# Reordering fills, the last chunk's normalisation and the merge in a one-core decoder block

## The chip, the cores and the metric

The kernel runs on one core of one Trainium2 chip. The metric is device time in microseconds (us): the time of one execution of the whole program, inputs and outputs in device memory. The time of the kernel before is the median of three runs; beside it stands one profiled execution with its own time.

## The reference

All arrays are float32, batch 1, 1024 tokens, model width 1024. Cut to what matters here:

```
xn   = rmsnorm(x, norm_pre_g)
u_a, z_a, o_a, i_a, f_a, u_b, z_b, g_pre = split(xn @ w_in)

# branch a: four mLSTM heads of width 256, chunks of 128 tokens (eight chunks)
c = silu(causal_conv4(u_a));  q, k from c;  v from u_a          # per head
S = (q k^T) * decay                     # inside a chunk
h = (S v + inter * C_prev q) / max(|den|, exp(-m))
C = a * C_prev + (decayed v)(k)         # matrix state, carried from chunk to chunk
h = sigmoid(o_a) * h;  h = h * rsqrt(mean(h*h) + eps)           # per head and token
y_a = ((h * head_g + skip * c) * silu(z_a)) @ w_a_out
# branch b: complex diagonal state space, gated, projected
y_b = s5(u_b, z_b) @ w_b_out
# merge
merged = sigmoid(g_a) * y_a + sigmoid(g_b) * y_b
out    = x + rmsnorm(merged @ w_o, norm_post_g)
```

## The kernel before

Every large product is made of pairs of fp32r values: a weight or an activation w is split into a high part (a copy on ScalarE) and a low part (a subtraction), and `dot3` issues three matmuls, high*high, high*low, low*high (L182 to L184). A projection unit of 512 tokens by 128 channels over eight row blocks is 24 such matmuls of 512 columns.

**Order.** The order of all work is written out by hand. A *unit* is one block of a projection; `run` executes it: it first sends pending stores and weight fetches to the queue of SyncE (SP), then the loads of the next `look[0]` units in `fillers`, then whatever stands in `early`, then the body, then what an earlier unit has deferred (`defer`, `step2`). `fill(n)` runs the next n units of the list `fillers`. All DMAs are issued by SP, in program order.

**Weights.** `plan` lists the weight blocks in order of use. `fetch` loads the next block into raw buffers (`wr`, two), `pump` splits it into `wh` (ScalarE, L142) and `wl` (VectorE, L144; GpSimd for later pieces where `pl` is set), two buffers each. `take` hands a block to its user, and with `ahead` pumps the next one.

**Heads.** The loop at L1273 runs over four heads, the inner loop at L1301 over eight chunks. For chunk c, `attn_a(c)` makes the scores, the decayed keys (`ksh`, `ksl`) and the scaled queries; `attn_b(c)` multiplies them with the values and with the state of the chunks before, updates the state and starts the output `hr`. Chunk c+1's `attn_a` is issued ahead of chunk c's `attn_b`. In between stand fills, which for heads 0 to 2 are the projection units of the next head (`o_unit`, eight token blocks, 24 matmuls of 256 columns; each writes a `sow` tile, of which there are two, and stores it). Before the change a head's first chunks go: fill, `attn_a(0)`, fill, `attn_a(1)`, `attn_b(0)`, fill, fill, `attn_a(2)`, `attn_b(1)`. After the eighth chunk come the `late` units of the next head: `u` (the convolution), `k`, `v`, `u`, `v`.

**Normalisation.** For each chunk `attn_ss` squares `hr` on ScalarE; after every fourth chunk GpSimd makes the scale `ss` from it and `attn_c` (VectorE, L1174, four instructions) applies it. `attn_ss` is deferred by one unit, `attn_c` stands in `early` and so runs ahead of the unit after that. `attn_d` (L1184, transposes on TensorE into PSUM, then VectorE) and `attn_e` (ScalarE, GpSimd L1204) turn the four chunks into rows of the input of w_a_out; for heads 0 to 2 they are stored to `yh_d`, `yl_d` and loaded back during head 3 (`ystep`).

**y_a and the merge.** w_a_out is used in two parts: `ya_unit` multiplies its first six row blocks (heads 0 to 2), while head 3 still runs, and stores gate * result + 0.25 * branch b to `pa_d`; `mg_unit` multiplies the last two row blocks (k = 6, 7; block `ya3`), adds `pa_d`, and splits the result into `mh`, `ml` (ScalarE L1366, GpSimd L1367, deferred by one unit). Column blocks 0 to 5 of `ya_unit` run as fills of head 3; blocks 6 and 7 (block `("ya", 3)`) run after it, mixed with the merge units: ya, mg, mg, ya, mg, mg, ya, mg, mg, ya, and then ten more `mg`. Results of projections go to a ring of three PSUM banks (`bank`), those of the heads mostly to a ring of five (`mbank`). `wo_unit(i, t)` is the last projection, four column blocks i by eight token blocks t, 24 matmuls of 256 columns each; at i = 3 it makes the norm's scale on VectorE (L1391, L1392) and GpSimd (L1393, a power), and `finish` scales, adds x and stores.

The lines that issue the merge before the change:

```
for m, hf in ((0, 0), (1, 0), (0, 1), (1, 1)):
    yaf(m, hf); mgf(*todo.popleft()); mgf(*todo.popleft())
```

Of the kernel before, what the change touches and what calls it, by code (L numbers as in the profile page):

```python
# [36 lines left out]
def hybrid_block(ctx, tc, x, norm_pre_g, w_in, conv_w, conv_b, w_q, w_k, w_v, b_i, b_f, head_g,  # L37
# [1077 lines left out]
    def attn_b(h, c):  # L1115
        hf, cl = c // 4, c % 4
        sh, sl_, qh, ql, ksh, ksl = hst.pop((h, c))
        vh, vl = vt[h, hf][0][:, cl, :], vt[h, hf][1][:, cl, :]
# [4 lines left out]
        if c < NCH - 1:
            for m in range(2):
                pc = mbank()
                ms = slice(m * P, (m + 1) * P)
# [24 lines left out]
        hr = ht((P, DH), "hr", 5)  # L1151
        sg = so.pop((h, c))
        V.scalar_tensor_tensor(hr, sg, 1.0, o[:, :DH], op0=ALU.add, op1=ALU.mult)
        hrs = hst["hr"]
        hrs.append(hr)
        if c < NCH - 1:
            tt(cl_, cf, ch_.bitcast(F32), ALU.subtract)
            ctm["hl"] = (ch_, cl_)
        defer(lambda: attn_ss(c, sg, hr, hrs, rd, ss))

    def attn_ss(c, sg, hr, hrs, rd, ss):
        cl = c % 4
# [56 lines left out]
            SY.dma_start(yh[k][:, HS[hf]].bitcast(F32), yh_d[k * P:(k + 1) * P, HS[hf]])  # L1219
            SY.dma_start(yl[k][:, HS[hf]].bitcast(F32), yl_d[k * P:(k + 1) * P, HS[hf]])  # L1220

    yaux = {}

    def ya_pre(ct, hf, pool=None):
        rs = slice(ct * P, (ct + 1) * P)
        pool, a, b, n = (hp, "hlh", "hll", 5) if pool is None else (pool, "ft", "fpa", 7)
        t1 = pool.tile([P, 512], F32, tag=a, bufs=n, name="y_t1")
        SY.dma_start(t1, t1_d[rs, HS[hf]])
        gb = pool.tile([P, 512], F32, tag=b, bufs=n, name="y_gb")
        SY.dma_start(gb, gb_d[rs, HS[hf]])  # L1230
        yaux[ct, hf] = (t1, gb)

    def ya_unit(i, m, hf):
        if m == 0 and hf == 0 and i < 3:
            cur["ya"] = take(("ya", i), i > 0)
        ct = 2 * i + m
        rs = slice(ct * P, (ct + 1) * P)
        t1, gb = yaux.pop((ct, hf))
        o = bank()
        proj_cm(o, cur["ya"], m * P, yh, yl, HS[hf], ks=list(range(6)))  # L1240
        V.scalar_tensor_tensor(t1, t1, 1.0, o, op0=ALU.add, op1=ALU.mult)
        V.scalar_tensor_tensor(gb, gb, 0.25, t1, op0=ALU.mult, op1=ALU.add)
        store(pa_d[rs, HS[hf]], gb)
# [29 lines left out]
    for h in range(H):  # L1273
# [81 lines left out]

    def mg_unit(ct, hf):
        if ct == 0 and hf == 0:
            cur["ya3"] = take("ya3", False)
        t1, pr = maux.pop((ct, hf))
        o = bank()  # L1360
        proj_cm(o, cur["ya3"], ct * P, yh, yl, HS[hf], ks=[6, 7])
        V.scalar_tensor_tensor(t1, t1, 1.0, o, op0=ALU.add, op1=ALU.mult)
# [3 lines left out]
        A.activation(mh[ct, hf], t1, AF.Copy)  # L1366
        defer(lambda: PL.tensor_tensor(ml[ct, hf], t1, mh[ct, hf].bitcast(F32), op=ALU.subtract))  # L1367

    ob, xres = {}, {}
    sso = fp.tile([P, NCH, 4], F32, name="sso")  # L1370

    def wo_unit(i, t):
        if t == 0:
# [12 lines left out]
        jk = fp.tile([P, 256], F32, tag="fjk", bufs=2, name="fjk")  # L1386
        A.activation(jk, o[:, :256], AF.Square, accum_out=sso[:, t, i:i + 1])
        mul(ob[t][:, cs], o[:, :256], gpo[:, cs])
        if i == 3:
            s = fp.tile([P, 1], F32, tag="fs", bufs=4, name="fs")  # L1390
            V.tensor_reduce(s, sso[:, t, :], axis=mybir.AxisListType.X, op=ALU.add)  # L1391
            V.tensor_scalar(s, s, 1.0 / D, 4.0 * EPS, op0=ALU.mult, op1=ALU.add)  # L1392
            PL.tensor_tensor(s, s, halfm[:, 0:1], op=ALU.pow)  # L1393
            finish(t, s)

# [65 lines left out]
```

## Time and profile before

| | |
|---|---|
| median of 3 runs | 996.41 us (995.38 to 998.93) |
| the profiled execution: its own time | 994.43 us |
| its span, first to last instruction | 992.7 us |
| TensorE busy | 971.8 us (98%) |
| VectorE, ScalarE, GpSimd busy | 625.5, 351.8, 203.1 us |
| granted TensorE clock, mean | 0.999 |
| moved by DMA | 148.32 MB, mean 149 GB/s |

How to read the rows that follow. A row of the timeline has the start in us from the beginning of the span, the duration, the engine, the line of the kernel, the operation, out<-in by tile names, partitions by elements, and in brackets how long the engine had been idle and what ended that. A row of the groups has the busy time and the mean duration of one instruction in ns, and then the idle time of the engine ahead of them. A row of the chain has start, duration and what it was. PE is TensorE, DVE VectorE, ACT ScalarE, POOL GpSimd, SPq the queue of SyncE. Matmuls overlap: a matmul of 512 columns shows about 0.40 us, but the next one starts earlier than that.

### The profile page before, as it was taken

To read this page: it belongs to the slowest core of one execution; us is meant where nothing else is said; L and a number is where in the kernel's file an instruction comes from. 1 tells how busy PE (TensorE), PEld (TensorE's weight loads), DVE (VectorE), ACT (ScalarE), POOL (GpSimd) and SP (SyncE) were. 2 spreads that over 40 slices of the span, in tenths; PEclk is the share of its full clock that TensorE was granted. 3 is DMA by queue.
4 is the path that set the end of the run, shared out by engine and by line. 5 is a ranking of instruction groups with operands and counts; after the bars stand their busy time and mean duration, and the time that the engine had idled before them with its cause. 6 is when DMAs were issued, how large, how long until landed. Compare 5 with 4: busy or idle time off the path is not lost.

```text
span 992.7 us, 15204 instructions
## 1 busy us (share of the span) xinstructions
PE 971.8 (98%) x5617; PEld 836.6 (84%) x5617; DVE 625.5 (63%) x1396; ACT 351.8 (35%) x696; POOL 203.1 (20%) x214
## 2 busy tenths in 40 slices
PE   7999999999999999999999999999999999999997
PEld 6878878888887789978998898889987888779997
DVE  4437978889644752435686667747774888765226
ACT  7312132331214421234544445435543442123311
POOL 4013222211122000012111321223221311343001
PEclk9999999999999999999999999999999999999999
DMA  7445323423334566114344253335446896783504
GB/s 256 111 130 158 112 88 97 109 58 107 108 100 164 185 216 226 59 64 151 96 133 152 85 173 122 134 95 179 130 151 189 270 312 204 268 299 121 191 1 170
DMA packets 115450, 148.32 MB, mean 149 GB/s; under 512 B 19080, under 2 KB 71472, under 8 KB 115376
## 3 DMA queue, kind: packets, MB, share of 16 engines
q1 hardware_dynamic: 115376, 147.35, 46.4%
q8 instruction: 44, 0.72, 0.3%
q14 instruction: 30, 0.25, 0.1%
HBM read 100.88 MB, written 46.43 MB: 148 GB/s over the span
## 4 chain that ended last, share of the span: by engine, by line
PE 85%; DVE 4%; DMA 4%; issue 3%; ACT 2%; POOL 1%; SPq 1%; DVEq 0%; POOLq 0%; ACTq 0%
PE pp L182 23%; PE pp L184 23%; PE pp L183 23%; PE pm L184 4%; PE pm L182 3%; PE pm L183 3%; DVE wl L144 1%; DMA wr<-in_w_in_dram 1%; PE pm L1088 1%; PE pm L664 1%; PE pm L705 1%; PE pm L704 1%; PE pm L1011 1%; DMA xt<-in_x_dram 1%; DMA ft<-t_d 1%
## 5 line engine op out<-in xcount | busy, mean ns | idle before, releaser
L182 PE MATMUL pp<-xh,wh 128*128 128x512 f32 x768 | 306.3, 399 | 3.3 <-DVE xl L278 2.5
L184 PE MATMUL pp<-xh,wl 128*128 128x512 f32 x768 | 303.6, 395 | 2.2 <-DVE wl L144 2.2
L183 PE MATMUL pp<-xl,wh 128*128 128x512 f32 x768 | 303.4, 395 | 0.2 <-DMA xl<-yl_d 0.2
L182 PEld LDWEIGHTS pp<-xh,wh 128*128 128x128 f32 x768 | 144.1, 188 | 39.9 <-DVE xl L278 2.8
L184 PEld LDWEIGHTS pp<-xh,wl 128*128 128x128 f32 x768 | 144.1, 188 | 37.9 <-DVE wl L144 3.1
L183 PEld LDWEIGHTS pp<-xl,wh 128*128 128x128 f32 x768 | 144.2, 188 | 33.2 <-DMA xl<-yl_d 0.7
L144 POOL TENSOR_TENSOR wl<-wr,wh 128x1024 fp32r<-128x1024 f32 (+1 forms) x25 | 61.6, 2481 | 227.3 <-ACT wh L142 227.3
L142 ACT ACTIVATE wh<-wr 128x1024 fp32r<-128x1024 f32 (+2 forms) x76 | 73.2, 1009 | 41.5 <-PE pm L183 30.6
L144 DVE TENSOR_TENSOR wl<-wr,wh 128x1024 fp32r<-128x1024 f32 (+2 forms) x51 | 59.9, 1207 | 21.7 <-ACT wh L142 17.2
L184 PE MATMUL pp<-wh,ml 128*128 128x256 f32 x256 | 72.2, 282 | 0.5 <-POOL ml L1367 0.5
L182 PE MATMUL pp<-wh,mh 128*128 128x256 f32 x256 | 72.1, 282 | 0.0
L183 PE MATMUL pp<-wl,mh 128*128 128x256 f32 x256 | 72.0, 281 | 0.0
L182 PE MATMUL pp<-wh,xh 128*128 128x256 f32 (+1 forms) x256 | 72.0, 281 | 0.0
L184 PE MATMUL pp<-wh,xl 128*128 128x256 f32 (+1 forms) x256 | 71.8, 280 | 0.0
L183 PE MATMUL pp<-wl,xh 128*128 128x256 f32 (+1 forms) x256 | 71.8, 280 | 0.0
L290 ACT ACTIVATE tg<-pp 128x512 f32<-128x512 f32 x32 | 19.2, 600 | 137.3 <-PE pp L184 94.3
L985 POOL TENSOR_TENSOR hll<-t2k,hlh 128x512 fp32r<-128x512 f32 x16 | 20.7, 1297 | 165.7 <-ACT hlh L984 89.1
L184 PEld LDWEIGHTS pp<-wh,ml 128*128 128x128 f32 x256 | 48.2, 188 | 0.7 <-POOL ml L1367 0.7
L182 PEld LDWEIGHTS pp<-wh,mh 128*128 128x128 f32 x256 | 48.2, 188 | 0.3 <-ACT mh L1366 0.2
L183 PEld LDWEIGHTS pp<-wl,xh 128*128 128x128 f32 x256 | 48.2, 188 | 0.2
L183 PEld LDWEIGHTS pp<-wl,mh 128*128 128x128 f32 x256 | 48.2, 188 | 0.1
L182 PEld LDWEIGHTS pp<-wh,xh 128*128 128x128 f32 x256 | 48.0, 188 | 0.2
(395 smaller groups left out, 1797.4 us busy)
## 6 DMA issues: line engine op xcount, KB each, us to landing
wr<-in_w_in_dram SPq DMA_DIRECT2D x48, 512.0 KB
t_d<-tg SPq DMA_DIRECT2D x32, 256.0 KB
xt<-in_x_dram SPq DMA_DIRECT2D x8, 512.0 KB
aux<-t_d SPq DMA_DIRECT2D x16, 256.0 KB
gb_d<-aux SPq DMA_DIRECT2D x16, 256.0 KB
so_d<-sow SPq DMA_DIRECT2D x32, 128.0 KB
sz_d<-t2k SPq DMA_DIRECT2D x16, 256.0 KB
cs_d<-t2k SPq DMA_DIRECT2D x16, 256.0 KB
```

What stands on the lines that cost most here:

```text
L142: A.activation(hi, raw, AF.Copy)
L144: eng.tensor_tensor(wl[:, k0:k0 + n, c0:c0 + w], raw, hi.bitcast(F32), op=ALU.subtract)
L182: PE.matmul(o, lh, rh, start=first, stop=False)
L183: PE.matmul(o, lh, rl, start=False, stop=False)
L184: PE.matmul(o, ll, rh, start=False, stop=last)
L290: A.activation(t, o, AF.Tanh, scale=0.5)
L664: PE.matmul(o[NS * b2:NS * (b2 + 1), g * P:(g + 1) * P], q["wt"][:, ri, g, NS * b2:NS * (b2 + 1)], ut[b][:, 2 * g + b2, :], start=True, st ...
L704: PE.matmul(o, m0[:, 2 * g + b2, :], ut[b][:, 2 * g + b2, :], start=True, stop=False)
L705: PE.matmul(o, vs[:, b2, g].rearrange("p t n -> p (t n)"), ss_[:, b2, g, :], start=False, stop=True)
L985: PL.tensor_tensor(lo, acc, hi.bitcast(F32), op=ALU.subtract)
L1011: PE.matmul(pm[:, 256 * k:256 * k + 256], wt[:, e, 256 + P * k:256 + P * k + P], wt[:, e, 0:256], start=e == 0, stop=e == 1)
L1088: PE.matmul(sc[:, :P], k_[:, m, sl], q_[:, m, sl], start=m == 0, stop=m == 1)
```

## The change

Nothing is added to or taken from the matmuls. The parts:

- **Chunk 0 of heads 0 to 2.** Two fills run ahead of `attn_a(1)` and `attn_b(0)` in place of one, and the fill after `attn_b(0)` goes; the count of fills per head stays.
- **Chunk 7 of each head.** `attn_ss` runs at once in place of being deferred by a unit, so `attn_c` runs ahead of the first unit after it. For head 2, `attn_d` of the second half then stands one unit earlier (after the `k` unit in place of the first `v` unit).
- **Blocks 6 and 7 of y_a.** Their `ya_unit` leaves its sum open in PSUM (`last=False`) and `mg_unit` goes on in the same bank. Their two VectorE instructions, their store to `pa_d` and the loads back go; the merge of these two reads gate and branch b from the tiles that the `ya_unit` loaded (`fyt`, `fyg`).
- **Order of the merge.** Two `ya`, six `mg`, two `ya`, six `mg`, then the last four `mg` in pairs between the first two `wo_unit`. Loads are issued four units ahead in place of three.
- **Weights.** The second piece of `ya3` is split on GpSimd; the fetch of the second w_o block comes after the merge's second run; its split one `wo_unit` later.
- **The norm.** Three of the four partial sums are added on VectorE one column block earlier; at i = 3 GpSimd adds the last one, and the two VectorE instructions there go. The squares' unused output has one buffer in place of two.

```diff
+        if c == NCH - 1:
+            attn_ss(c, sg, hr, hrs, rd, ss)
+        else:
+            defer(lambda: attn_ss(c, sg, hr, hrs, rd, ss))
...
-        pool, a, b, n = (hp, "hlh", "hll", 5) if pool is None else (pool, "ft", "fpa", 7)
+        pool, a, b, n = (hp, "hlh", "hll", 5) if pool is None else (pool, "fyt", "fyg", 2)
...
-        proj_cm(o, cur["ya"], m * P, yh, yl, HS[hf], ks=list(range(6)))
+        proj_cm(o, cur["ya"], m * P, yh, yl, HS[hf], ks=list(range(6)), last=i < 3)
+        if i == 3:
+            maux[ct, hf] = (t1, gb, o)
+            return
...
-            fill()
+            fill(2 if c == 0 and h < H - 1 else 1)
...
-            if c % 4 != 3 if h < H - 1 else c in (2, 4, 6):
+            if c in ((1, 2, 4, 5, 6) if h < H - 1 else (2, 4, 6)):
                 fill()
...
-            if i == (3 if h < H - 2 else 2):
+            if i == (3 if h < H - 2 else 1):
                 attn_d(h, 1)
...
-    cur["ya"] = take(("ya", 3))
+    cur["ya"] = take(("ya", 3), False)
+    pump(pl=True)
...
-        pr = fp.tile([P, 512], F32, tag="fpa", bufs=7, name="fpa")
+        pr = fp.tile([P, 512], F32, tag="fpa", bufs=5, name="fpa")
...
-        t1, pr = maux.pop((ct, hf))
-        o = bank()
-        proj_cm(o, cur["ya3"], ct * P, yh, yl, HS[hf], ks=[6, 7])
+        t1, pr, o = maux.pop((ct, hf))
+        part = o
+        o = bank() if part is None else part
+        proj_cm(o, cur["ya3"], ct * P, yh, yl, HS[hf], ks=[6, 7], first=part is None)
         V.scalar_tensor_tensor(t1, t1, 1.0, o, op0=ALU.add, op1=ALU.mult)
-        tt(t1, t1, pr, ALU.add)
+        if part is None:
+            tt(t1, t1, pr, ALU.add)
+        else:
+            V.scalar_tensor_tensor(t1, pr, 0.25, t1, op0=ALU.mult, op1=ALU.add)
...
-        A.activation(jk, o[:, :256], AF.Square, accum_out=sso[:, t, i:i + 1])
+        A.activation(jk, o[:, :256], AF.Square, scale=1.0 / 32.0, accum_out=sso[:, t, i:i + 1])
         mul(ob[t][:, cs], o[:, :256], gpo[:, cs])
+        if i == 2:
+            V.tensor_reduce(sso[:, t, 4:5], sso[:, t, 0:3], axis=mybir.AxisListType.X, op=ALU.add)
+            V.tensor_scalar(sso[:, t, 4:5], sso[:, t, 4:5], 4.0 * EPS, None, op0=ALU.add)
         if i == 3:
-            V.tensor_reduce(s, sso[:, t, :], axis=mybir.AxisListType.X, op=ALU.add)
-            V.tensor_scalar(s, s, 1.0 / D, 4.0 * EPS, op0=ALU.mult, op1=ALU.add)
+            PL.tensor_tensor(s, sso[:, t, 3:4], sso[:, t, 4:5], op=ALU.add)
             PL.tensor_tensor(s, s, halfm[:, 0:1], op=ALU.pow)
...
-    todo = deque((ct, hf) for hf in range(2) for ct in range(KT))
-    for m, hf in ((0, 0), (1, 0), (0, 1), (1, 1)):
-        yaf(m, hf)
-        mgf(*todo.popleft())
-        mgf(*todo.popleft())
-    for ct, hf in todo:
+    yaf(0, 0)
+    yaf(1, 0)
+    for ct in (6, 7, 0, 1, 2, 3):
+        mgf(ct, 0)
+    yaf(0, 1)
+    yaf(1, 1)
+    n_ya = len(fillers)
+    for ct, hf in ((6, 1), (7, 1), (4, 0), (5, 0), (0, 1), (1, 1)):
         mgf(ct, hf)
-    look[0] = 3
+    n_hf = len(fillers) - n_ya
+    for ct in range(2, 6):
+        mgf(ct, 1)
+    look[0] = 4
...
-    fill(10)
+    fill(n_ya)
     pump()
-    fill(4)
+    pending.pop()
+    fill(n_hf)
+    pending.append(fetch)
     for t in range(NCH):
         run(unit(lambda: wo_unit(0, t)))
-        fill(3)
-        if t == 1:
+        fill(2)
+        if t == 2:
             pump()
```

More of the change, by code (lines that the diff above doesn't have):

```diff
@@ L1158, in attn_b @@
             ctm["hl"] = (ch_, cl_)
-        defer(lambda: attn_ss(c, sg, hr, hrs, rd, ss))
+        if c == NCH - 1:
+            attn_ss(c, sg, hr, hrs, rd, ss)
+        else:
+            defer(lambda: attn_ss(c, sg, hr, hrs, rd, ss))
     def attn_ss(c, sg, hr, hrs, rd, ss):
@@ L1220, in ystep @@
             SY.dma_start(yl[k][:, HS[hf]].bitcast(F32), yl_d[k * P:(k + 1) * P, HS[hf]])
-    yaux = {}
+    yaux, maux = {}, {}
     def ya_pre(ct, hf, pool=None):
         rs = slice(ct * P, (ct + 1) * P)
-        pool, a, b, n = (hp, "hlh", "hll", 5) if pool is None else (pool, "ft", "fpa", 7)
+        pool, a, b, n = (hp, "hlh", "hll", 5) if pool is None else (pool, "fyt", "fyg", 2)
         t1 = pool.tile([P, 512], F32, tag=a, bufs=n, name="y_t1")
@@ L1345, in hybrid_block @@
     mh, ml = {}, {}
-    maux = {}
     def mg_pre(ct, hf):
@@ L1351, in mg_pre @@
         SY.dma_start(t1, t1_d[rs, HS[hf]])
-        pr = fp.tile([P, 512], F32, tag="fpa", bufs=7, name="fpa")
+        pr = fp.tile([P, 512], F32, tag="fpa", bufs=5, name="fpa")
         SY.dma_start(pr, pa_d[rs, HS[hf]])
-        maux[ct, hf] = (t1, pr)
+        maux[ct, hf] = (t1, pr, None)
     def mg_unit(ct, hf):
-        if ct == 0 and hf == 0:
+        if "ya3" not in cur:
             cur["ya3"] = take("ya3", False)
-        t1, pr = maux.pop((ct, hf))
-        o = bank()
-        proj_cm(o, cur["ya3"], ct * P, yh, yl, HS[hf], ks=[6, 7])
+        t1, pr, o = maux.pop((ct, hf))
+        part = o
+        o = bank() if part is None else part
+        proj_cm(o, cur["ya3"], ct * P, yh, yl, HS[hf], ks=[6, 7], first=part is None)
         V.scalar_tensor_tensor(t1, t1, 1.0, o, op0=ALU.add, op1=ALU.mult)
-        tt(t1, t1, pr, ALU.add)
+        if part is None:
+            tt(t1, t1, pr, ALU.add)
+        else:
+            V.scalar_tensor_tensor(t1, pr, 0.25, t1, op0=ALU.mult, op1=ALU.add)
         mh[ct, hf] = fp.tile([P, 512], F32R, name=f"mh{ct}{hf}")
@@ L1369, in hybrid_block @@
     ob, xres = {}, {}
-    sso = fp.tile([P, NCH, 4], F32, name="sso")
+    sso = fp.tile([P, NCH, 5], F32, name="sso")
     def wo_unit(i, t):
@@ L1385, in wo_unit @@
         cs = slice(256 * i, 256 * (i + 1))
-        jk = fp.tile([P, 256], F32, tag="fjk", bufs=2, name="fjk")
-        A.activation(jk, o[:, :256], AF.Square, accum_out=sso[:, t, i:i + 1])
+        jk = fp.tile([P, 256], F32, tag="fjk", bufs=1, name="fjk")
+        A.activation(jk, o[:, :256], AF.Square, scale=1.0 / 32.0, accum_out=sso[:, t, i:i + 1])
         mul(ob[t][:, cs], o[:, :256], gpo[:, cs])
+        if i == 2:
+            V.tensor_reduce(sso[:, t, 4:5], sso[:, t, 0:3], axis=mybir.AxisListType.X, op=ALU.add)
+            V.tensor_scalar(sso[:, t, 4:5], sso[:, t, 4:5], 4.0 * EPS, None, op0=ALU.add)
         if i == 3:
             s = fp.tile([P, 1], F32, tag="fs", bufs=4, name="fs")
-            V.tensor_reduce(s, sso[:, t, :], axis=mybir.AxisListType.X, op=ALU.add)
-            V.tensor_scalar(s, s, 1.0 / D, 4.0 * EPS, op0=ALU.mult, op1=ALU.add)
+            PL.tensor_tensor(s, sso[:, t, 3:4], sso[:, t, 4:5], op=ALU.add)
             PL.tensor_tensor(s, s, halfm[:, 0:1], op=ALU.pow)
@@ L1403, in mgf @@
     def mgf(ct, hf):
-        fillers.append(unit(lambda: mg_unit(ct, hf), lambda: mg_pre(ct, hf)))
+        fillers.append(unit(lambda: mg_unit(ct, hf), lambda: (ct, hf) in maux or ct > 5 or mg_pre(ct, hf)))
     def yaf(m, hf):
         fillers.append(unit(lambda: ya_unit(3, m, hf), lambda: ya_pre(6 + m, hf, fp)))
-    todo = deque((ct, hf) for hf in range(2) for ct in range(KT))
-    for m, hf in ((0, 0), (1, 0), (0, 1), (1, 1)):
-        yaf(m, hf)
-        mgf(*todo.popleft())
-        mgf(*todo.popleft())
-    for ct, hf in todo:
-        mgf(ct, hf)
-    look[0] = 3
-    for i in range(3):
+    yaf(0, 0)
[6 more added lines that the diff above has]
+    for ct, hf in ((6, 1), (7, 1), (4, 0), (5, 0), (0, 1), (1, 1)):
+        mgf(ct, hf)
+    n_hf = len(fillers) - n_ya
+    for ct in range(2, 6):
+        mgf(ct, 1)
+    look[0] = 4
+    for i in range(4):
         fillers[i][0]()
         fillers[i] = (None,) + fillers[i][1:]
-    fill(10)
+    fill(n_ya)
     pump()
-    fill(4)
+    pending.pop()
+    fill(n_hf)
+    pending.append(fetch)
     for t in range(NCH):
         run(unit(lambda: wo_unit(0, t)))
-        fill(3)
-        if t == 1:
+        fill(2)
+        if t == 2:
             pump()
```

## The prediction

> **What bounds the kernel now.** I read the page's first parts, then the waits of TensorE, then the timeline around each of them.
>
> ```profile
> span 992.7 us, 15204 instructions
> ...
> PE 971.8 (98%) x5617; PEld 836.6 (84%) x5617; DVE 625.5 (63%) x1396; ACT 351.8 (35%) x696; POOL 203.1 (20%) x214
> ```
>
> TensorE is busy for 98% of the span, and the change takes no matmul away. Only TensorE's waits can be won, and the tail after its last matmul. These are the waits that the change touches, in TensorE's timeline, with four successive matmuls that give a wait's price:
>
> ```profile
> 474.05 0.36 PE L182 MATMUL pm<-vh,ksh 128*128 128x258 f32 x1 [0.65 <-issue]
> ...
> 576.58 0.39 PE L182 MATMUL pm<-vh,ksh 128*128 128x258 f32 x1 [0.74 <-ACT ksh L1102]
> ...
> 577.40 0.39 PE L184 MATMUL pm<-vh,ksl 128*128 128x258 f32 x1 [0.31 <-DVE ksl L1107]
> ...
> 679.47 0.39 PE L182 MATMUL pm<-vh,ksh 128*128 128x258 f32 x1 [0.75 <-ACT ksh L1102]
> ...
> 680.28 0.39 PE L184 MATMUL pm<-vh,ksl 128*128 128x258 f32 x1 [0.32 <-DVE ksl L1107]
> ...
> 766.51 1.46 PE L1184 MATMUL pm<-ident,hr 128*128 128x128 f32 x8 [1.46 <-DVE hr L1174]
> ...
> 794.91 0.50 PE L183 MATMUL pp<-xl,wh 128*128 128x512 f32 x1 [0.17 <-DMA xl<-yl_d]
> ...
> 855.41 0.39 PE L183 MATMUL pp<-xl,wh 128*128 128x512 f32 x1
> 856.78 0.50 PE L184 MATMUL pp<-xh,wl 128*128 128x512 f32 x1 [0.98 <-DVE wl L144]
> 857.11 0.40 PE L182 MATMUL pp<-xh,wh 128*128 128x512 f32 x1
> 857.35 0.40 PE L183 MATMUL pp<-xl,wh 128*128 128x512 f32 x1
> 859.00 0.50 PE L184 MATMUL pp<-xh,wl 128*128 128x512 f32 x1 [1.26 <-DVE wl L144]
> ...
> 883.53 0.50 PE L182 MATMUL pp<-xh,wh 128*128 128x512 f32 x1 [0.23 <-DVE ft L1362]
> ...
> 888.42 0.39 PE L184 MATMUL pp<-wh,ml 128*128 128x256 f32 x1 [0.51 <-POOL ml L1367]
> ...
> 892.14 0.50 PE L182 MATMUL pp<-xh,wh 128*128 128x512 f32 x1 [0.53 <-DVE ob L442]
> ```
>
> A matmul of 512 columns follows the one before after 0.24 us (857.11 to 857.35). Around the first `wl` wait it is 1.37 (855.41 to 856.78), and 0.33 for the next: 1.22 lost for 0.98 shown. So a wait costs its bracket plus 0.25. That makes 0.90 at head 0's chunk 0, 1.55 and 1.57 at those of heads 1 and 2, 1.71 at head 2's `attn_d`, 0.42 at the load of `yl_d`, 2.74 for `ya3`'s two low pieces, 0.48, 0.76 and 0.78 later in the merge: 10.9 us, 1.1% of the span. That is the ceiling, before the tail.
>
> **Chunk 0, two fills ahead.** The fill brought forward stands between head h's first scores and the matmuls that wait for `ksh`, `ksl`. Rows of head 2:
>
> ```profile
> 677.83 0.68 DVE L442 TENSOR_TENSOR vl<-pp,vh 128x512 fp32r<-128x512 f32 x1
> ...
> 683.44 0.69 DVE L442 TENSOR_TENSOR ctl<-ct,cth 128x516 fp32r<-128x516 f32 x1
> ```
> ```profile
> 677.90 0.60 PE L1088 MATMUL pm<-q,k 128*128 128x128 f32 x4
> ...
> 681.23 0.28 PE L182 MATMUL pp<-wh,xh 128*128 128x256 f32 x1
> ...
> 686.88 0.38 PE L1088 MATMUL pm<-q,k 128*128 128x128 f32 x2
> ```
> ```profile
> 670.69 3.60 DMA wr<-in_w_in_dram
> ```
> ```profile
> 681.13 0.88 SPq L82 DMA_DIRECT2D so_d<-sow  x2
> ```
> ```profile
> 681.17 0.31 ACT L1096 ACTIVATE sTh<-sT 128x128 fp32r<-128x128 f32 x1 [0.96 <-DVE sT L442]
> ```
>
> Two fills now run from 681.23 to 686.88, so one is 2.8 us. The moved one would begin at 677.90, and `ksl` (needed by 680.28 now) would be asked for at about 681.3: the old wait is covered by 1 us. But the fill itself gets new waits. Its PSUM bank, third in the ring of three, is that of the last `v` unit, whose `vl` VectorE reads until 678.51: 0.6 late, with the price 0.7 (estimate; head 1 alike, head 0 none, its VectorE is ahead). Second, it is the third writer of `sow`, of which there are two, so ScalarE must wait until the first one's store, issued at 681.13, has landed. No row shows this landing; it lies between the issue and, at worst like the load of 512 KB, four times its size, 3.60 later, at 684.7. Behind that wait on ScalarE stand `sTh`, `ksh`, `q2h` and the state's copies of the next chunk; from `sTh` to the end of `ctl` it now takes 2.96 (681.17 to 684.13). ScalarE comes to `sTh` at 682.4, when the later scores allow it, or at 685.5, when the store lands last and two instructions (0.8, an estimate) go first; so `ctl` is done at 685.3 to 688.5. TensorE asks for it after another fill, scores and values, at about 687.8. So 0 to 0.9 is lost here; I take 0.3, nearer the early end, since the store is small. SP itself moves nothing by this: its order stays, and the cs_d store and the loads of `cz` keep their place. Gain: 0.90 + (1.55 - 1.0) + (1.57 - 1.0) = 2.0, between 0.9 and 4.0.
>
> **Chunk 7 at once, `attn_d` earlier.**
>
> ```profile
> 760.09 0.69 DVE L442 TENSOR_TENSOR hll<-pp,hlh 128x512 fp32r<-128x512 f32 x1 [4.54 <-ACT hlh L952]
> ...
> 764.93 2.21 DVE L1174 TENSOR_SCALAR hr<-hr,ss 128x256 f32<-128x256 f32 x4
> ```
> ```profile
> 762.17 0.20 POOL L1165 TENSOR_SCALAR ss<-ss 128x4 f32<-128x4 f32 x1 [18.96 <-ACT so L1163]
> ```
> ```profile
> 789.51 5.36 DMA xl<-yl_d
> ```
>
> Now `attn_c` ends at 767.1, behind the convolution on VectorE. Moved, its chain (the square, three small GpSimd operations) begins right after chunk 7's `hr`, and the four instructions fall into VectorE's idle 4.54 ahead of 760.09. The transposes then stand one `v` unit earlier (24 matmuls of 256 columns, 2.8) and ask at about 762.2: ready two microseconds before. What is queued behind `attn_c` is the next `u` unit's `hll` at 760.09; if the cover went, that unit's bank would be read 1 to 2 later, with two banks still free. So 1.71 goes. The stores of `yh_d`, `yl_d` and the loads behind them on SP move forward with `attn_d` by one unit, more than the 1.71 by which TensorE comes earlier, so the 0.42 at the landing (789.51 + 5.36) goes too. Gain 2.1, between 1.0 and 2.1. In the other heads `attn_d` keeps its place: nothing.
>
> **The merge.**
>
> ```profile
> L142 ACT ACTIVATE wh<-wr 128x1024 fp32r<-128x1024 f32 x66 | 66.6, 1054 | 30.6 <-PE pm L183 19.7 <-PE pp L183 7.0 <-DMA wr<-in_w_in_dram 3.3
> ...
> L1367 POOL TENSOR_TENSOR ml<-ft,mh 128x512 fp32r<-128x512 f32 x16 | 23.8, 1510 | 23.4 <-ACT mh L1366 23.4
> ...
> L144 DVE TENSOR_TENSOR wl<-wr,wh 128x1024 fp32r<-128x1024 f32 x42 | 52.8, 1289 | 21.7 <-ACT wh L142 17.2 <-PE pm L184 4.5
> ...
> L442 DVE TENSOR_TENSOR ft<-ft,fpa 128x512 f32<-128x512 f32 x16 | 13.3, 829 | 0.6
> ...
> L1366 ACT ACTIVATE mh<-ft 128x512 fp32r<-128x512 f32 x16 | 10.1, 633 | 34.6 <-DVE ft L442 34.6
> ...
> L1362 DVE SCALAR_TENSOR_TENSOR ft<-ft,pp 128x512 f32<-128x512 f32 x16 | 10.9, 684 | 2.6 <-DMA ft<-t_d 2.3 <-PE pp L184 0.3
> ```
> ```profile
> 854.41 4.54 DVE L144 TENSOR_TENSOR wl<-wr,wh 128x1024 fp32r<-128x1024 f32 x2
> ...
> 875.71 1.82 DVE L442 TENSOR_TENSOR ft<-ft,fpa 128x512 f32<-128x512 f32 x1
> ...
> 889.19 0.69 DVE L1362 SCALAR_TENSOR_TENSOR ft<-ft,pp 128x512 f32<-128x512 f32 x1 [1.96 <-DMA ft<-t_d]
> ```
>
> `ya3`'s low pieces are done at 858.95 and asked for from 855.6, after one `ya` unit. A second `ya` unit in front (18 matmuls by 0.235, 4.2) asks for them at 859.9, and GpSimd takes one of the two pieces. Even if VectorE's piece ended only at 859, the 2.74 goes.
>
> What is late next is VectorE. A merge unit is six matmuls, 1.40; VectorE's pair on it is 0.68 + 0.83 = 1.51. Before, a `ya` unit after every two gave it time; now six merge units come in a row. The first run ends in 8.4 us of `ya` units, in which VectorE has nothing to do: no loss. The second run starts with w_o's split, which gets its buffer when the last `ya` unit ends: ScalarE 1.05, then VectorE 2 x 1.29, so the first pair starts 3.6 after that. The fourth unit's bank, which `wo_unit` takes, is free at 3.6 + 3 x 1.51 + 0.68 = 8.8, asked for at 8.4: 0.65 with the price. Its `ml` is ready at 3.6 + 4 x 1.51 + 0.63 + 1.51 = 11.8; `wo_unit` wants it as the 18th matmul (0.118 apart), at 11.1: 0.95. So 1.6 in place of 0.48 + 0.76 + 0.78 = 2.02.
>
> Four stores and eight loads of 256 KB go, 3 MB, and none of the loads waits for a store of this stage any more, so the late load of 889.19 goes. Against it, the loads of the first run now stand behind w_o's fetch on SP, which waits for `ya3`'s split. They would land near 865 (a landing takes 5.4 above), and the first bank that hangs on one is asked for at 866.4 (859.4 and five merge units): nothing, up to 1 us. VectorE's dropped instructions are no gain by themselves. Merge: 2.74 + 2.02 - 1.6 = 3.2, between 0 and 4.8.
>
> **The norm's tail.**
>
> ```profile
> 986.71 0.19 ACT L1387 ACTIVATION_READ_ACCUMULATOR fjk<-pp 128x1 f32 x1
> ```
> ```profile
> 987.75 0.54 POOL L1393 TENSOR_TENSOR fs<-fs,halfm 128x1 f32<-128x1 f32 x1 [2.31 <-DVE fs L1392]
> ```
>
> Between 986.90 and the power at 987.75 lie 0.85 of VectorE's work and hand-over. A GpSimd add takes its place; it is not shown, at most as long as the power, 0.54, plus 0.1 of hand-over. Gain 0.2 to 0.75; I take 0.4. The two VectorE instructions at i = 2 and the single square buffer, which ScalarE alone writes, cost nothing beside 24 matmuls.
>
> **Sum.** 2.0 + 2.1 + 3.2 + 0.4 = 7.7 us. The profiled execution's 994.43 becomes 986.7; the median of the runs, 996.41, lies 1.98 above it, so a median of 988.7.
>
> **Rivals.**
> - *VectorE and GpSimd shut each other out in the merge.* The add of 875.71 took 1.82 against 0.69 at best, while GpSimd made an `ml`. If each pair took 0.68 + 1.82 = 2.5 against TensorE's 1.40 with three banks, the first run loses about 1.3, the second 5.0, together 6.3 in place of my 1.6: 993.4. For it: in a run of six, `ml` follows `ml`. Against it: the mean add is 0.83.
>   The Trainium skill, page "SBUF — State Buffer", section "SBUF: two separate sides", speaks for it: it calls the port pair of VectorE and GpSimd an exclusive lock, held for a whole instruction, when VectorE reads two SBUF inputs; the add does, the operation on PSUM does not. The trace agrees for the add of 1.82, and its mean says that the full price is rare.
> - *Chunk 0 gains nothing*: the two new waits take what the old one gave: 990.7.
> - *The waits only move*, to the next late engine, all over: 996.4. Against it: VectorE is busy for 63%.
> - *Slower: ScalarE hangs on the `so_d` store.* If it lands like the load of `yl_d` or later, `ctl` comes at 681.13 + 5.36 + 0.8 + 2.96 = 690.3 in place of 687.8: 2.5 lost per head. It decides for slower only if three heads lose over 3.6 more than I take, a landing after 6.8 or so: three times 4.0 gives 988.7 + 12 = 1000.7. Against it: the store has little ahead of it in the queue.
>
> **How the numbers follow.** The forecast, 985 to 991.5: 0.66. Shut out in the merge: 0.10. Chunk 0 for nothing: 0.12. Only moved: 0.08. Slower: 0.04. About 0.3%, 3 us, is what a measurement here can tell from no change: below 993.4 is faster. That takes the forecast, chunk 0 for nothing and half of the shut-out case, whose 993.4 lies on the bound: 0.83. Same has the other half and the moved waits: 0.13. The range runs from the ceiling with the tail (996.4 - 10.9 - 0.75, near 984.8, less some spread) to just above the shut-out case: 984 to 994.
>
> **What would show it.** Right: no TensorE wait at L182, L184 on `ksh`, `ksl`; none at L1184 on `hr`; none on `wl`; a new short wait of the first fills on `vl`; ScalarE's `sow` waiting for a DMA in heads 1 and 2; a wait of the first `wo_unit` on `ml`; the power starting about 0.4 after the accumulator's read. Wrong: waits of TensorE summing to over 5 us after 850, adds in the merge of 1.3 and more throughout, or `ctl` ending waits at chunk 1.

## The result, and the profile after

The changed kernel takes 988.9 us in the median of six runs (987.70 to 989.98), the kernel before, beside it, 995.9: a ratio of 0.9928 (95% interval 0.9916 to 0.9940). Measured again beside its variants it was 0.9932 (0.9920 to 0.9945). The forecast was 988.7, between 984 and 994. The profiled execution took 989.22, its span is 987.5, and the page's first lines are:

```profile
span 987.5 us, 15179 instructions
...
PE 972.2 (98%) x5617; PEld 839.6 (85%) x5617; DVE 621.5 (63%) x1387; ACT 351.8 (36%) x696; POOL 209.7 (21%) x223
```

TensorE is as busy as before; the time came out of its waits. Those that are left in the stages of the change, in its timeline (start, duration, line, tiles, and in brackets the wait and who ended it):

```profile
575.34 0.38 PE L182 MATMUL pp<-wh,xh 128*128 128x256 f32 x1 [0.31 <-ACT sow L839]
...
583.75 0.44 PE L1100 MATMUL pm<-ident,k 128*128 128x128 f32 x2 [0.30 <-DVE ksl L1107]
...
585.12 0.36 PE L182 MATMUL pm<-vh,sTh 128*128 128x258 f32 x1 [0.20 <-DVE hr L1153]
...
678.25 0.39 PE L182 MATMUL pp<-wh,xh 128*128 128x256 f32 x1 [0.32 <-ACT sow L839]
...
687.74 0.35 PE L182 MATMUL pm<-vh,sTh 128*128 128x258 f32 x1 [0.22 <-DVE hr L1153]
...
883.83 0.39 PE L184 MATMUL pp<-wh,ml 128*128 128x256 f32 x1 [0.25 <-POOL ml L1377]
...
885.51 0.39 PE L184 MATMUL pp<-wh,ml 128*128 128x256 f32 x1 [1.06 <-POOL ml L1377]
```

No wait on `ksh` at 474, 576, 679, none on the normalised `hr` at 766, none on `yl_d`, `wl`, `ft`, `ob`. In their place stand three kinds: the third fill of heads 1 and 2 waits for a bank (575.34, 678.25), chunk 1 of these heads is late (583.75, 585.12, 687.74), and the first `wo_unit` waits for `ml`. For chunk 0 and chunk 7 the table compares the time between the same two score matmuls (L1088) in the two traces: from chunk 0's to chunk 4's in each head, from chunk 7's of head 2 to chunk 0's of head 3 (the transposes), and from chunk 2's to chunk 7's of head 3 (the load). The merge is priced as in the prediction, by the distance from start to start above the usual one:

| | forecast | in the two profiled executions |
|---|---|---|
| chunk 0 | 2.0 | 1.4 (head 0: 1.15; head 1: -0.03; head 2: 0.25) |
| chunk 7, `attn_d`, `yl_d` | 2.1 | 2.7 (2.05 at the transposes, 0.64 at the load) |
| merge, waits | 3.2 | 2.8 (4.74 before, 1.97 left) |
| norm's tail | 0.4 | 0.3 (last matmul to the end 6.65, now 6.31) |
| `wo_unit`'s matmuls, 118.7 to 120.0 ns apart | not seen | -1.0 |
| sum | 7.7 | 6.2 |

The spans differ by 5.2 only, because this execution comes to head 0 some 1.0 us later than that of before, by work that the change does not touch: its first 25 us lost 9.0 us, those of before 7.6, and over the profiled executions of all runs here it is 7.0 to 10.4. The waits there are alike in the two (5.8 us of idle time each). What differs is the granted clock, which stood at one half from 16.5 to 20.0 us in this execution. The same 2 us of both traces (busy time, matmuls, granted clock, DMA share, GB/s), before and then the changed kernel:

```profile
17.00:19.00 2.00, 2.00 (x11) 1.00 1.02 390
```
```profile
17.00:19.00 2.00, 2.00 (x7) 0.50 1.03 375
```

The medians, 7.0 and 6.6 apart, fit the 6.2.

The distance of `wo_unit`'s matmuls was not in the forecast's account. ScalarE squares each result of `wo_unit` (L1387 before, L1397 after), so its rows mark every 24th matmul. In the timeline of before, 28 units lie between these two rows:

```profile
906.68 0.39 ACT L1387 ACTIVATE fjk<-pp 128x256 f32<-128x256 f32 x1 [1.06 <-PE pp L184]
...
986.42 0.38 ACT L1387 ACTIVATE fjk<-pp 128x256 f32<-128x256 f32 x1 [2.37 <-PE pp L184]
```

and of the changed kernel 26 between these:

```profile
906.69 0.38 ACT L1397 ACTIVATE fjk<-pp 128x256 f32<-128x256 f32 x1 [2.40 <-PE pp L184]
...
981.56 0.38 ACT L1397 ACTIVATE fjk<-pp 128x256 f32<-128x256 f32 x1 [2.40 <-PE pp L184]
```

79.74 / 28 is 2.848 us for a unit before, 74.87 / 26 is 2.880 now: without any wait, each matmul follows the one before after 120.0 ns, not 118.7. Times 768, that is 1.0 us.

### The profile page after: what moved, and what is told of

It is laid out like the page before. It is cut to its first block, busy times and chain, and to the rows that moved or that the text cites. A ratio compares the mean times of both kernels' runs of the same rounds, so it can differ in the third digit from the quotient of the medians.

```text
span 987.5 us, 15179 instructions
## 1 busy us (share of the span) xinstructions
PE 972.2 (98%) x5617; PEld 839.6 (85%) x5617; DVE 621.5 (63%) x1387; ACT 351.8 (36%) x696; POOL 209.7 (21%) x223
## 4 chain that ended last, share of the span: by engine, by line
PE 88%; issue 3%; DMA 3%; POOL 3%; DVE 2%; ACT 1%; SPq 0%; DVEq 0%; POOLq 0%; ACTq 0%
PE pp L182 24%; PE pp L184 23%; PE pp L183 23%; PE pm L182 4%; PE pm L184 4%; PE pm L183 4%; PE pm L1088 1%; DMA wr<-in_w_in_dram 1%; POOL wl L144 1%; PE pm L664 1%; PE pm L705 1%; PE pm L704 1%; PE pm L1011 1%; POOL ml L1377 1%; DMA xt<-in_x_dram 1%
## 5 line engine op out<-in xcount | busy, mean ns | idle before, releaser
L144 POOL TENSOR_TENSOR wl<-wr,wh 128x1024 fp32r<-128x1024 f32 (+1 forms) x26 | 64.1, 2480 | 233.1 <-ACT wh L142 233.1
L144 DVE TENSOR_TENSOR wl<-wr,wh 128x1024 fp32r<-128x1024 f32 (+2 forms) x50 | 57.0, 1172 | 26.3 <-ACT wh L142 21.7
```

The source lines that it names most:

```text
L144: eng.tensor_tensor(wl[:, k0:k0 + n, c0:c0 + w], raw, hi.bitcast(F32), op=ALU.subtract)
```

## The experiments

Where not said otherwise an edit is made to the changed kernel, and the ratio is to the kernel before on the same chip.

**Chunk 0 undone.**

```
-            fill(2 if c == 0 and h < H - 1 else 1)
+            fill()
...
-            if c in ((1, 2, 4, 5, 6) if h < H - 1 else (2, 4, 6)):
+            if c % 4 != 3 if h < H - 1 else c in (2, 4, 6):
```

> The changed kernel with the fills of chunk 0 put back (one fill ahead, one behind). Theory: the two fills are worth 1.6 us, nearly all in head 0 (1.15 there, 0.1 in head 1, 0.4 in head 2), because heads 1 and 2 pay two new waits. So about 990.5, TensorE's waits on ksh and ksl back at chunk 0 of heads 0, 1 and 2 (brackets 0.65, 0.74 and 0.75, and 0.3 twice on ksl), its waits for the third fill's bank and on hr and ksl at chunk 1 gone. Rival: the forecast's 2.0 us or more, 990.9 and above, if the new waits cost only what was forecast. Rival: nothing, 988.9, if head 0's wait went for another reason.

Measured: 990.31, ratio 0.9932 (0.9916 to 0.9949), which by itself cannot be told from the changed kernel's. Its TensorE timeline has the waits back, here head 2's:

```profile
680.77 0.39 PE L182 MATMUL pm<-vh,ksh 128*128 128x258 f32 x1 [0.74 <-ACT ksh L1102]
...
681.59 0.39 PE L184 MATMUL pm<-vh,ksl 128*128 128x258 f32 x1 [0.32 <-DVE ksl L1107]
```

From chunk 0's scores to chunk 4's this run takes, in each of the three heads, what the kernel before takes, to 0.01 us. The changed kernel is shorter there by 1.4 in sum, in its second profile by 1.7, and by 1.8 and 1.9 in two variants that leave this part as it is (eight units ahead, low pieces on VectorE). ScalarE's wait for the store of `so_d` is 3.4 to 3.7 in the first of these profiles and 3.3 to 3.4 in the variants, so the part is worth 1.4 to 1.9, more as that store lands sooner; the rival of 2.0 and more falls.

**Chunk 7 undone.**

```
-        if c == NCH - 1:
-            attn_ss(c, sg, hr, hrs, rd, ss)
-        else:
-            defer(lambda: attn_ss(c, sg, hr, hrs, rd, ss))
+        defer(lambda: attn_ss(c, sg, hr, hrs, rd, ss))
...
-            if i == (3 if h < H - 2 else 1):
+            if i == (3 if h < H - 2 else 2):
```

> The changed kernel with chunk 7's normalisation deferred again and head 2's attn_d one unit later. Theory: both of the waits that went come back, 1.7 to 1.9 us at the transposes of hr and 0.4 to 0.6 at the load of yl_d: 2.1 to 2.6, so about 991.3. Rival: only the wait on hr comes back, because the load of yl_d now finds a queue with less ahead of it: 1.9, 990.8. Rival: the transposes' wait was only moved before, nothing comes back: 988.9.

Measured: 991.74, ratio 0.9946 (0.9929 to 0.9963), span 991.0. TensorE's timeline:

```profile
766.17 1.46 PE L1184 MATMUL pm<-ident,hr 128*128 128x128 f32 x8 [1.46 <-DVE hr L1174]
...
795.32 0.50 PE L183 MATMUL pp<-xl,wh 128*128 128x512 f32 x1 [0.17 <-DMA xl<-yl_d]
```

Both waits are back: 1.92 at `hr`, and 1.4 at the load, where several matmuls came late, not one as before the change. 3.3 in all; the theory's 2.6 was too little.

**The old merge.** All of it as before the change; the tail stays new. Its core:

```
-    yaf(0, 0)
-    yaf(1, 0)
-    for ct in (6, 7, 0, 1, 2, 3):
-        mgf(ct, 0)
...
+    for m, hf in ((0, 0), (1, 0), (0, 1), (1, 1)):
+        yaf(m, hf)
+        mgf(*todo.popleft())
+        mgf(*todo.popleft())
```

> The changed kernel with the whole merge of before (its order, its four stores and loads of y_a's last column blocks, three loads ahead, both low pieces of ya3 on VectorE). Theory: the two waits on wl come back (2.8 us) and the three of 0.5 to 0.8 (2.0), against 2.05 of the new order that go: 2.8 slower, about 991.7, with 3 MB more moved. Rival: the forecast's sizes, 3.2: 992.1. Rival: VectorE and GpSimd shut each other out so much in the new order that the old one is hardly worse: within 1 us of 988.9.

Measured: 992.72, ratio 0.9950 (0.9933 to 0.9968), span 991.3. The two waits on `wl` are back, and here they cost more than themselves:

```profile
854.08 0.50 PE L184 MATMUL pp<-xh,wl 128*128 128x512 f32 x1 [0.99 <-DVE wl L144]
...
856.30 0.80 PE L184 MATMUL pp<-xh,wl 128*128 128x512 f32 x1 [1.27 <-DVE wl L144]
856.90 0.63 PE L182 MATMUL pp<-xh,wh 128*128 128x512 f32 x1
857.33 0.63 PE L183 MATMUL pp<-xl,wh 128*128 128x512 f32 x1
```

The next matmuls come 0.43 apart in place of 0.235. The table by stretches (busy time, matmuls, granted clock, DMA share, GB/s) shows the clock halved over the 2.8 us of its second row:

```profile
850.00:856.00 6.00, 4.05 (x17) 0.98 1.00 307
856.40:859.20 2.80, 2.80 (x7) 0.50 1.07 384
859.30:865.00 5.70, 5.70 (x26) 1.00 1.01 380
```

That is 1.3 us beside the waits. In the kernel before, the same pair of waits left the clock at 1.00. With it the old merge costs 5.5 against 1.97, 3.5 more; without it 2.2.

**Low pieces of `ya3` both on VectorE**, in the new order.

```
-    pump(pl=True)
+    pump()
```

> The changed kernel with the low pieces of ya3 both on VectorE as before the change, the order of the merge being the new one. Theory: the second y_a unit in front is what took the wait on wl away, not GpSimd's share: VectorE's add of 849.34, which took 2.68 us beside GpSimd's 2.40 us piece, takes 0.69 to 1.0 again, so VectorE comes to its first piece 1.7 to 2 us earlier and is done with both at about 856, when TensorE asks for them: within 0.3 us of the changed kernel, no wait on wl of over 0.2. Rival: without GpSimd VectorE is late by a piece: the second is done at 858, and TensorE waits 1.3 us or more on wl.

Measured: 989.19, ratio 0.9930 (0.9913 to 0.9947), TensorE without any wait on `wl`. VectorE's timeline:

```profile
849.39 4.56 DVE L144 TENSOR_TENSOR wl<-wr,wh 128x1024 fp32r<-128x1024 f32 x2
```

Both pieces are done at 853.95. In the changed kernel VectorE does one, and ends it later:

```profile
849.34 2.68 DVE L442 TENSOR_TENSOR t2k<-t2k,cz 128x512 f32<-128x512 f32 x1
...
853.33 2.32 DVE L144 TENSOR_TENSOR wl<-wr,wh 128x1024 fp32r<-128x1024 f32 x1
```

The second `ya_unit` in front took the wait away; GpSimd's share gave nothing, since its piece of 2.40 us held VectorE's small add up by 2.0.

**Eight merge units ahead of the second pair of `ya_unit`.**

```
-    for ct in (6, 7, 0, 1, 2, 3):
+    for ct in (6, 7, 0, 1, 2, 3, 4, 5):
...
-    for ct, hf in ((6, 1), (7, 1), (4, 0), (5, 0), (0, 1), (1, 1)):
+    for ct, hf in ((6, 1), (7, 1), (0, 1), (1, 1)):
```

> The changed kernel with the merge units (4, 0) and (5, 0) moved ahead of the second pair of y_a units, so that eight merge units run first and the second run has four. Theory: the 2.05 us of TensorE's waits at 881 to 886 (0.24 on the bank, 0.5 and 1.3 on ml) are those of ml of (4, 0) and (5, 0), which GpSimd makes last; now they are made during the 8.4 us of y_a units, the waits go, and it is 2.0 us faster than the changed kernel; up to 0.4 may come back as bank waits in the run of eight. Rival: GpSimd and VectorE shut each other out (GpSimd 1.6 us for an ml, VectorE 1.07 for an add in place of 0.69): a run of eight falls behind by 0.3 a unit and waits for its banks, at 868 to 872, by 1 us or more, so that half of the gain is lost.

Measured: 986.43, ratio 0.9898 (0.9884 to 0.9912), 3.3 below the changed kernel on the same chip (989.77). No wait on `ml` and none on a bank is left; its summary of TensorE's waits (who for whom, total, times, longest) goes straight from the kernel's head to chunk 1:

```profile
PE pp L336 <- POOL halfm L77: 1.4, 1, 1.4
PE pp L182 <- ACT sow L839: 0.6, 2, 0.3
PE pm L182 <- DVE hr L1153: 0.4, 2, 0.2
```

The gain of the step is the 1.9 in the trace. The medians differ by more; this profile lost only 7.0 in the first 25 us, but how much of the rest of the 3.3 that makes up in the other runs is not shown. The rival falls: the adds took 1.07 beside GpSimd, and a run of eight did not fall behind by a bank.

**Three `sow` buffers.**

```
-        t = ht((P, DH), "sow", 2)
+        t = ht((P, DH), "sow", 3)
```

> The changed kernel with three buffers for sow in place of two; the kilobyte for it comes from the small tiles of the gates, which now lie in buffers that chunk 0 uses later. Theory: ScalarE's wait of 3.42 us for the store of so_d is what makes chunk 1 of heads 1 and 2 late; it goes, and with it TensorE's waits there on ksl and hr, 0.9 in head 1 and 0.5 in head 2: 1.4 to 1.5 faster than the changed kernel, about 987.4. The wait of the third fill's first matmul (0.58 in each of the two heads) stays. Rival: chunk 1 is late by VectorE (sTl took 1.30 in place of 0.29 while GpSimd made hll): ScalarE's wait goes, TensorE's waits stay, 988.9.

Measured: 985.96, ratio 0.9893 (0.9875 to 0.9910), more than forecast. ScalarE's wait and every wait of TensorE at chunk 1 are gone. What these looked like in the changed kernel, on ScalarE:

```profile
677.83 0.36 ACT L839 ACTIVATE sow<-pp 128x256 f32<-128x256 f32 x1
...
683.49 0.39 ACT L839 ACTIVATE sow<-pp 128x256 f32<-128x256 f32 x1 [3.42 <-DMA so_d<-sow]
```

and on VectorE behind it:

```profile
684.62 1.30 DVE L442 TENSOR_TENSOR sTl<-sT,sTh 128x128 fp32r<-128x128 f32 x1 [2.17 <-ACT sTh L1096]
...
687.51 0.69 DVE L442 TENSOR_TENSOR ctl<-ct,cth 128x516 fp32r<-128x516 f32 x1
```

With three buffers `sTl` still takes 1.29 beside GpSimd, but starts at 679.50: VectorE's slow instruction alone does not make TensorE wait, the rival falls.

**The same places, two `sow` buffers.** The tiles had moved with the third buffer, and the span was shorter by 4.0, not 1.4. On top of that kernel:

```
-        t = ht((P, DH), "sow", 3)
+        if c == 0 and h == 0:
+            ht((P, DH), "sow2", 1)
+        t = ht((P, DH), "sow", 2)
```

> The changed kernel with every tile at the place that it has in the one with three sow buffers, but sow itself with two (the third lies idle). It parts what the third buffer does from what the moved tiles do. Theory: of the 4.0 us by which the span of the three-buffer kernel is shorter, 1.5 to 1.9 come from chunk 1 of heads 1 and 2, 0.8 from the qkv and value matmuls (232.7 to 229.5 ns apart for 512 columns, 117.7 to 114.3 for 256) at their new place, and the rest from the head of the kernel, which differs from run to run. So this one keeps the 0.8, has ScalarE's wait of 3.4 us and TensorE's waits on ksl and hr again, and is about 0.8 us faster than the changed kernel. Rival: the third buffer does it all, the matmuls' distance too (through what ScalarE and VectorE read beside them): 117.7 again, as slow as the changed kernel.

Measured: 988.35, ratio 0.9921 (0.9909 to 0.9934), against 989.77 of the changed kernel beside it. ScalarE waits 3.29 again, TensorE at chunk 1 too: from chunk 0's scores to chunk 4's heads 1 and 2 take 0.94 and 0.63 us more than with three buffers at the same places, which is what the third buffer is worth. But the value matmuls keep their new distance. The first and the twelfth of half a unit, in the changed kernel:

```profile
670.04 0.28 PE L182 MATMUL pp<-wh,hlh 128*128 128x256 f32 x1
...
671.33 0.28 PE L184 MATMUL pp<-wh,hll 128*128 128x256 f32 x1
```

and in this one:

```profile
669.18 0.28 PE L182 MATMUL pp<-wh,hlh 128*128 128x256 f32 x1
...
670.42 0.28 PE L184 MATMUL pp<-wh,hll 128*128 128x256 f32 x1
```

1.29 against 1.24 for eleven steps; over all of them the mean is 117.7 against 114.3 ns, and for the 512-column matmuls that read `hlh` 232.7 against 229.5. Nothing but the places of tiles differs: `hlh`, `hll` begin 64 bytes above a multiple of 256, where they had begun 192 above.

**The changed kernel again**, for comparison.

> The changed kernel itself, beside its variants on the same chip. Both theories expect a ratio of 0.993 to the kernel before, the waits of the first profile to within 0.1 us, and matmuls of w_o 120.0 ns apart.

Measured: 989.77, ratio 0.9932 (0.9920 to 0.9945), the same waits, 120.0 ns.

**`sso` eight wide.** The changed kernel made `sso` five wide, and `mh`, `ml`, which lie behind it, had moved: 128 bytes above a multiple of 256 before, 160 now.

```
-    sso = fp.tile([P, NCH, 5], F32, name="sso")
+    sso = fp.tile([P, NCH, 8], F32, name="sso")
```

> The changed kernel with sso 8 elements wide in place of 5 (the last three unused), so that mh and ml, which lie behind it, start at multiples of 64 bytes as before the change, and not 32 bytes off. Theory: the matmuls of w_o, 120.0 ns apart in the changed kernel and 118.7 before it, are slower because of where mh and ml lie; they go back to 118.7, which is 767 times 1.3 ns, 1.0 us: about 0.1% faster than the changed kernel. Rival: they are slower because more is loaded beside them (113 GB/s in place of 99 in the stretch from 900 to 975 us): they stay at 120.0, no change.

Measured: 988.90, ratio 0.9928 (0.9914 to 0.9941); the distance stays at 120.0. That a multiple of 64 bytes is enough falls: 0 above a multiple of 256 is as slow as 160. The rival's outcome came, but its reason does not follow: in the run with the old merge, where `sso` is five wide too, `mh`, `ml` lie at 160, 103 GB/s are moved in that stretch, near the 99 of before, and the distance is 120.0 as well.

**`sso` ten wide.**

```
-    sso = fp.tile([P, NCH, 5], F32, name="sso")
+    sso = fp.tile([P, NCH, 10], F32, name="sso")
```

> The changed kernel with sso 10 elements wide, so that mh and ml start 64 bytes above a multiple of 512, where the value matmuls' stationary tiles lay when they came 114.3 ns apart in place of 117.7; their moving operands are the same two buffers of wh and wl. In the runs so far w_o's matmuls are 118.7 apart (128 above a multiple of 256), 120.0 (160 above) and 120.0 (0). Theory: the distance follows from where the stationary tile lies relative to the moving one: 114.3 to 115, 768 times 5 ns, 3.8 to 4.3 us faster than the changed kernel, about 985. Rival: the value matmuls' gain has to do with their short accumulations of six, or with what ran beside them: w_o's stay between 118.5 and 120, at most 1 us.

Measured: 984.28, ratio 0.9876 (0.9859 to 0.9893). 26 units lie between these two of ScalarE's rows:

```profile
905.79 0.39 ACT L1397 ACTIVATE fjk<-pp 128x256 f32<-128x256 f32 x1 [2.25 <-PE pp L184]
...
976.51 0.38 ACT L1397 ACTIVATE fjk<-pp 128x256 f32<-128x256 f32 x1 [2.25 <-PE pp L184]
```

70.72 / 26 / 24 is 113.3 ns. No less is moved beside them than in the changed kernel (125 GB/s against 113 from 900 to 975 us), so the loads were not it. A number in a shape that nothing computes with is worth 5 us.

**Copies of `attn_e` one unit later**, on top of three buffers.

```
-        defer(lambda: attn_e(h, hf, ts_))
+        defer(lambda: attn_e(h, hf, ts_), 2 if hf and h < H - 2 else 1)
```

> The kernel with three sow buffers, and in heads 0 and 1 the second half's attn_e (ScalarE's two copies, GpSimd's two subtractions, four stores) deferred by one unit more, so that on ScalarE the tanh of the next head's first fill stands ahead of those copies. It asks what the third fill's first matmul waits for (0.49 and 0.11 us in each of heads 1 and 2). The program puts the third fill into the PSUM bank of the first fill, and the trace names the first fill's sow, which ends at 678.19, 0.06 ahead of that matmul. Theory: it waits for this tanh, which stands behind attn_e's copies; now the wait goes, 1.2 us faster than with three buffers alone (986.0). Rival, the forecast's reason: it waits for vl of the last value unit on VectorE, where nothing changes: the wait stays, 986.0.

Measured: 985.48, ratio 0.9889 (0.9870 to 0.9908). The wait of the third fill is gone from both heads, 1.2 us of TensorE; the medians show less of it, and in this profile the first 25 us lost 10.4, with the clock at one half for 6.8 us. ScalarE's timeline has the order turned:

```profile
673.59 0.38 ACT L839 ACTIVATE sow<-pp 128x256 f32<-128x256 f32 x1 [2.27 <-PE pp L184]
674.95 0.63 ACT L1203 ACTIVATE t2k<-t2k 128x512 fp32r<-128x512 f32 x1 [0.97 <-DVE t2k L442]
```

**Everything together.** The edits of the three buffers, the copies, the eight units and `sso` ten wide, and:

```
+    main.tile([P, 96], F32, name="gap_a")
     xh = [main.tile([P, L], F32R, tag=f"xh{k}", name=f"xh{k}") for k in range(KT)]
...
-    par = main.tile([P, 80], F32, name="par")[:, 0:NPAR]
+    par = main.tile([P, 112], F32, name="par")[:, 0:NPAR]
```

> Everything together: the changed kernel with three sow buffers, the copies of attn_e one unit later, eight merge units ahead of the second pair of y_a units, mh and ml 64 bytes above a multiple of 512, and, new, xh and xl (now 192 above one) moved to 64 above it too, wh and wl staying where they are. (For the room, tri shares ksh's place and ScalarE's unused squares in the w_o stage are bfloat16; no sum changes by it.) Theory: the waits add: from 989.2, the middle of the changed kernel's medians, 1.3 for the third buffer, 1.2 for the copies, 1.9 for the eight ahead, 4.5 for mh, 0.8 for the qkv and value matmuls at their new place: 979.5. And if the distance of matmuls follows from where the tiles lie, those of xh change as those of hlh did when hlh went from 192 to 64: o's from 117.6 to about 114.3 (576 of them, 1.9 us), the 2304 of 512 columns from 233.0 to about 229.5, 8 us: about 970. Rival: for xh, whose 512 columns come as the moving operand from a row of 1024, the place makes no difference: 979.5. Rival: each part's gain is given back by the next wait, as in the change itself: 982 or more.

Measured: 970.34, ratio 0.9746 (0.9732 to 0.9759). The page's first lines:

```profile
span 967.3 us, 15184 instructions
...
PE 954.4 (99%) x5617; PEld 831.1 (86%) x5617; DVE 621.0 (64%) x1387; ACT 352.2 (36%) x696; POOL 211.9 (22%) x223
```

As many matmuls as in the changed kernel, and TensorE busy for 17.8 us less. The 2304 of 512 columns on `xh` are 229.4 ns apart, 233.2 in the changed kernel (8.8 us); the 576 of `o_unit` 114.9, 117.7 there (1.6); `w_o`'s 113.3 (5.1). Of the rest some 1.6 is the half-speed stretch at 16.5 us in the changed kernel's profile, which this execution did not have. The value matmuls came at about 116, not 114.3, with `hlh` at 64 as in the three-buffer kernel: the place of that one tile does not settle the distance alone. `wh` and `wl` did not stay where they were, as the expectation has it: with the two edits above they lie 512 bytes further. Whether that is the reason was not tried.

## Why the prediction was right, step by step

- *Chunk 0, two fills.* Head 0's gain and both new waits came as forecast, with the total 0.6 lower: in head 1 the new waits took back all that the old one gave, in head 2 most of it. **The bank's wait** was sized right (0.58 against 0.7) and put down to the wrong instruction: not `vl` of the last value unit, as a ring of three banks counted in turn would have it. The program gives the third fill the first fill's bank, and the experiment with the copies one unit later shows what held it: that fill's tanh, behind `attn_e`'s copies on ScalarE. **The store's wait** was seen in its place; the price of 0.3 was too low, the third buffer takes away 0.94 and 0.63. ScalarE came on some 2.5 after the store's issue at 681.01, inside the bounds, but `ctl` ended at 688.2, near the late one: `sTl` took 1.30 beside GpSimd, in place of the 0.29 that the 2.96 from `sTh` to `ctl` had in it. TensorE was held by what comes out on the way there, `ksl` and `hr`.
- *Chunk 7.* Both waits gone, 2.05 for 1.71 and 0.64 for 0.42: the bracket plus 0.25 is short where several matmuls in a row come late.
- *Merge.* The waits on `wl` went; "GpSimd takes one of the two pieces" was no part of it, as the run with both pieces on VectorE shows. What is left is the order with its second `ya` unit in front; the other parts of the new merge were undone only together with it. The new wait on `ml` was forecast with 0.95 and measured 1.8, the bank's with 0.65 and measured 0.1: the sum, 1.97 for 1.6, was kinder than its parts. Most of the adds took 1.05 to 1.08 where I had put 0.83.
- *Tail.* GpSimd's add took 0.19, and the power started 0.35 after the accumulator's read (forecast 0.4); no run undid the tail alone, its 0.3 is read from the trace:

```profile
982.11 0.19 POOL L1404 TENSOR_TENSOR fs<-sso 128x1 f32<-128x1 f32 x1 [2.06 <-ACT fjk L1397]
982.38 0.54 POOL L1405 TENSOR_TENSOR fs<-fs,halfm 128x1 f32<-128x1 f32 x1
```

- *The sum* held because four terms were each off by 0.1 to 0.6, not all the same way, and the one that was missing, 1.0 for `sso`, was hidden in a difference of medians of 7.0. That 988.7 came within 0.2 of the median is luck: the 7.7 was 0.7 more than the medians differ by, and the 996.41 that it was taken from, a median of three runs, 0.5 more than the six runs give. The claim that the tail's new instructions "cost nothing beside 24 matmuls" is true of their time and false of their tile. "Only TensorE's waits can be won, and the tail" is false too: the last kernel took 17.8 us off TensorE's busy time with the same matmuls, more than the 10.9 of all the waits.
- *The rivals.* Of the lock between VectorE and GpSimd, the slow adds are there and the loss is not. ScalarE did hang on the store, for 3.4 us, but went on 2.5 after its issue, where 6.8 would have decided for slower.
  The Trainium skill ("SBUF — State Buffer", "SBUF: two separate sides") has the port pair held for a whole instruction. The 2.68 of the small add beside GpSimd's 2.40 agrees; the adds of 1.07 beside an `ml` of 1.6 lost 0.4, less than the instruction beside them.

## What to carry to other kernels

Price the waits that a new order creates by what stands ahead on the same in-order engine: here a third buffer, one deferred unit and two moved units took away what the change had left, each found as one bracket in the timeline. When TensorE is 98% busy, measure the distance between matmuls and the granted clock in each stage as well as its waits, before and after: a tile that changes its size moves all tiles behind it, and that can cost or give more than the schedule. Take the user of a buffer from the program, not from counting the ring.

## What the runs showed of the hardware

**Distance of matmuls and the place of their operands.** In `wo_unit`, same shapes, same loop: `mh`, `ml` at 128 above a multiple of 256 gave 118.7 ns, at 160 and at 0 120.0, at 64 113.3. At 160 the 120.0 is a mean of unlike steps: in the changed kernel 116.6 from a matmul with `mh` that reads a `wl` block at 768 above a multiple of 2048 to the next, and 124.5 from one that reads a `wh` block at 256. In the run with chunk 7 undone, with the same tiles at the same places, it is the other way round, 123.2 and 116.4, so the place alone does not say which step is the long one. At 0 all are 120.0. `xh` from 192 to 64, with `wh` and `wl` 512 bytes further: 233.2 to 229.4 at 512 columns. The places are those that the program gives its tiles; no trace shows them. 64 was the best place in all that was tried; the rule behind it stays open, and the value matmuls of the last kernel show that it has a second part.

**The clock.** In the run with the old merge two waits of 0.99 and 1.27 us, 2.2 apart, were followed by a granted clock of 0.50 from 855.8 to 859.3; the same pair in the kernel before was not. Near the start every kernel here has TensorE idle for 2.2 to 2.8 us, up to about 15 us: in eight of the fourteen profiled executions the clock went to one half there, for 3.4 us, once for 6.8, and in six it did not. The length of that wait does not part them (2.36 with it, 2.80 without). It shows in the times: of 38 runs of the kernel before beside the variants, the three with a granted clock of 0.999 took 994.5 us in the mean, the eight with 0.995 took 997.0. The Trainium skill ("TensorE: Matmul & The Clock Gate", "HAM oscillation — how this bites in real kernels") warns of gaps over some 3.4 us. No gap here was that long, and the two of the old merge not half as long; the measurement decides.
